# A hybrid convolution and neighbourhood-attention block: another ordering of the same instructions by the framework's scheduler

## The chip, the cores and the metric

The kernel runs on one core of one Trainium2 chip. The metric is the time of one execution on the device in microseconds (us); smaller is better. The engines of the core work in parallel, each through its own list of instructions in order: PE (TensorE: matmuls and transposes), DVE (VectorE: elementwise work), ACT (ScalarE: activations and copies), POOL (GpSimd) and SP (SyncE), the last two here only as issuers of transfers (DMA). An instruction starts when the one ahead of it on its engine is through and the semaphores that it waits for are reached.

## What is computed

One layer over 512 latent tokens of 1024 channels (a grid of 8 rows by 64 columns) with 256 context tokens. Cut to what matters:

```python
h  = _rmsnorm(x, pre_g)   * (1.0 + sc) + sh          # modulation from c
hc = _rmsnorm(ctx, pre_g) * (1.0 + sc_c) + sh_c      # context, modulation from c_ctx
parts = _split_in(h @ w_in)      # 10 parts of 1024: b, c, x_in, z_a, q, k, v, z_b, g_a, g_b
q, k = _apply_rope(_heads(parts[4]), cos, sin), _apply_rope(_heads(parts[5]), cos, sin)
k_c, v_c = split(hc @ w_in[:, K_OFF:V_END])
attn = _neighbourhood_attention(q, k, v, k_c, v_c, rpb)   # window 8 x 16 and all context keys, one softmax
y_a = (silu(z_a) * b * _dwconv3(c * x_in, conv_w, conv_b)) @ w_out_conv
y_b = (silu(z_b) * attn) @ w_out_attn
y   = (sigmoid(g_a) * y_a + sigmoid(g_b) * y_b) @ w_o
return x + gt * _rmsnorm(y, post_g)
```

There are 16 heads of 64 channels; the arithmetic is float32.

## The kernel before

**Precision.** A float32 operand is split in two parts, a high one `H` and a low one `L` (`split`, L64 to L72: ACT casts the high part at L67, or scaled at L70, and DVE takes the difference at L68, or L71). A product is three matmuls: high by high, high by low, low by high. So every weight and every activation costs one pass on ACT and one on DVE ahead of PE.

**Stages.** The prologue (to about 52 us) loads x, computes the modulation from `wmod` (tiles `wm`), transposes the normed x and multiplies the first weight slabs (`fraw`, cast to `fH` and `fL`) as they come: per slab k, ACT makes the modulated `m` (L516), splits it into `h` (L67), and PE multiplies (L422 to L426). For PE, DVE, ACT and SP this part stands inside `manual_schedule`, where the order is that of the code. The load of the rotary tables `cosin` (L554) stands behind that block in the code. Then come four blocks of the convolution branch; then the main part: a loop over 64 blocks (8 head pairs p, two heads h each, four query blocks b), in which each slot issues attention work of pair p and, in between, projection work for later pairs from `plan` (the fillers: `keys_queries`, `values`, `conv_pairs`, `gate2`, `merge_gates`); then the branch projections with the merge (from about 540 us), and the output projection with the closing norm (from about 664 us).

**Attention of one block.** `scores` (L715, or L724 for the fourth block b = 3): PE multiplies queries `qd`, `qe` by keys `ks` into a tile `ps` in one of two banks (`psS`); DVE adds the bias `bt` and takes the row maximum `m` (L731); ACT takes the exponential into `pt` (L738, L742), three buffers in all; after two blocks DVE takes the reciprocal of the sums `z` (L743) and ACT scales both (L745). `turn2` (L752): PE transposes `pt` into two banks (`psT`), and ACT and DVE split the result into `TH` and `TL` (L67, L68). `gather` (L771): twelve matmuls by the values `V` for the whole head; ACT copies (L776), DVE adds into `at` (L777, L778).

**Queries and keys.** `keys_queries` projects q and k for a later pair. For the pairs 3, 4 and 6 (and for some other projections) it goes through `pair` (L293 to L316), which saves multiplications by sums of blocks: products at L287 into three tiles, which ACT copies (L298, L301, L303, L309) and DVE combines (L304, L312, L315) into `tc`. `rope` (L619 to L625) multiplies by the tables on DVE (L621 into `tb`, L622 in place) and adds the swapped half by two accumulating transfers from POOL's queue (L624). After that ACT casts `qd` (L70) and `ks` (L67), and POOL's queue copies halves between tiles (L680, L681, L688 to L690) before the scores of that pair can start. `values` projects v at L175 and L180 (with `summed`, L205 and L206, and the split into `V`); the context's keys are projected at L194 and L199. `block_sums` (L594 to L598) makes the sums `S` of the activations that `pair` multiplies.

**The end.** `tokens` (L1006) multiplies merged activations by blocks of `w_o` for four token tiles t; `squares` (L1027 on ACT, L1028 on DVE) takes the sum of squares and scales; `added` (L1032) adds partial products; `partial` (L1038, L1040) and `close` (L1044 on ACT, L1045 and L1047 on DVE, the output at L1051) finish a tile.

**What sets the order.** Outside `manual_schedule` the code's order is only a proposal. The framework collects the instructions with their dependencies inside `tile.TileContext`, simulates them, and lays down the list of each engine in the order in which its simulation would run them; then it puts in the semaphores. Which simulation it takes is an argument of `TileContext` (L1197).

## Time and profile before

| what | us |
|---|---|
| median of three runs | 709.33 (709.26 to 709.7) |
| the profiled execution | 710.12 |
| its span | 708.3 |
| PE busy | 695.4 |
| DVE busy | 585.2 |
| ACT busy | 437.2 |
| POOL busy | 66.9 |

The profile is of one execution. The span goes from its first to its last instruction; the profiled execution's own time is 1.8 us longer and 0.8 us above the median. The parts that matter are: the busy times; the chain of work that ended last, followed back from the end; the table of what each engine waited for (time in total, times, longest); windows of time with each engine's busy time, PE's granted clock and the share and rate of the DMA engines; and the timeline, whose rows give start, duration, engine, line, operation, output and inputs, a count where equal rows are joined, and in brackets the idle time ahead and who ended it. Matmuls are pipelined, so a row's duration is longer than the distance to the next; prices per matmul are taken from start to start.

### The profile page before, as it was taken

What the parts mean: (1) busy time and instruction counts of PE and PEld (TensorE: products, weight loads), DVE (VectorE), ACT (ScalarE), POOL (GpSimd) and SP (SyncE); (2) the same over time, 40 slices, a digit from 0 to 9 for tenths busy, and PEclk for the clock granted to TensorE, in tenths of its full rate; (3) what the DMA queues carried; (4) which work ended last, traced back from release to release, by engine and by line L of the source; (5) the groups of instructions that cost most, each with busy time, mean ns of one, the idle gap of its engine ahead of it and who ended that gap; (6) DMA issues with size and microseconds to landing.
All of it is one profiled execution on the core that took longest, in us unless ns stands there. A gap on an engine that the chain in (4) does not pass through costs nothing.

```text
span 708.3 us, 11424 instructions
## 1 busy us (share of the span) xinstructions
PE 695.4 (98%) x4196; PEld 618.5 (87%) x4196; DVE 585.2 (83%) x1114; ACT 437.2 (62%) x868; POOL 66.9 (9%) x110
## 2 busy tenths in 40 slices
PE   7999999999999999999999999999999999999996
PEld 4888888888889989898999999999898899988885
DVE  6979997668599989978898797999799675665996
ACT  6566632656577678765886676888694444442563
POOL 0000002240130310401302103000000000000000
PEclk9999999999999999999999999999999999999999
DMA  8996896565341563642636436313733233570013
GB/s 341 407 348 228 281 339 172 134 163 143 100 99 29 137 157 119 151 125 61 168 106 171 94 127 154 104 60 98 250 115 120 88 119 120 186 261 30 31 59 120
DMA packets 37466, 108.27 MB, mean 153 GB/s; under 512 B 5025, under 2 KB 5281, under 8 KB 37410
## 3 DMA queue, kind: packets, MB, share of 16 engines
q1 hardware_dynamic: 28946, 92.20, 38.0%
q0 software_dynamic: 8320, 15.21, 10.7%
q8 instruction: 33, 0.54, 0.3%
q14 instruction: 23, 0.19, 0.1%
q10 hardware_dynamic: 144, 0.13, 0.1%
HBM read 87.07 MB, written 5.24 MB: 130 GB/s over the span
## 4 chain that ended last, share of the span: by engine, by line
PE 88%; DVE 5%; DMA 3%; ACT 2%; issue 1%; SPq 0%; POOL 0%; DVEq 0%; ACTq 0%
PE ps L287 23%; PE ps L162 11%; PE ps L163 11%; PE ps L164 11%; PE ps L175 6%; PE ps L1006 5%; PE ps L771 4%; PE ps L180 3%; PE ps L752 3%; PE ps L715 3%; PE ps L194 2%; PE ps L422 2%; PE ps L426 2%; PE ps L423 2%; DMA fraw<-in_wfirst 1%; DVE w L68 1%
## 5 line engine op out<-in xcount | busy, mean ns | idle before, releaser
L67 ACT CAST w<-raw 128x512 fp32r<-128x512 f32 (+1 forms) x193 | 137.2, 731 | 91.4 <-PE ps L164 30.7
L68 DVE TENSOR_TENSOR w<-raw,w 128x512 fp32r<-128x512 f32 (+1 forms) x193 | 156.3, 824 | 41.8 <-ACT w L67 41.0
L287 PE MATMUL ps<-S,w 128*128 128x256 f32 x960 | 122.0, 283 | 1.2 <-ACT tc L303 1.2
L287 PEld LDWEIGHTS ps<-S,w 128*128 128x128 f32 x960 | 118.1, 192 | 1.5 <-ACT tc L303 1.4
L287 PE MATMUL ps<-h,w 128*128 128x256 f32 x720 | 94.2, 284 | 0.5 <-DVE tc L315 0.4
L287 PEld LDWEIGHTS ps<-h,w 128*128 128x128 f32 x720 | 89.9, 191 | 2.5 <-DVE tc L315 0.9
L162 PE MATMUL ps<-h,w 128*128 128x512 f32 x208 | 81.5, 392 | 0.0
L164 PE MATMUL ps<-h,w 128*128 128x512 f32 x208 | 81.2, 390 | 0.0
L163 PE MATMUL ps<-h,w 128*128 128x512 f32 x208 | 81.0, 390 | 0.0
L624 POOL DMA_DIRECT2D tc<-tb x32 | 28.8, 1175 | 301.9 <-DVE tc L622 182.6
L164 PEld LDWEIGHTS ps<-h,w 128*128 128x128 f32 x208 | 39.0, 188 | 8.2
L67 ACT CAST TH<-ps 128x512 fp32r<-128x512 f32 x64 | 36.0, 588 | 16.5 <-PE ps L752 16.4
L162 PEld LDWEIGHTS ps<-h,w 128*128 128x128 f32 x208 | 39.1, 188 | 8.0
L163 PEld LDWEIGHTS ps<-h,w 128*128 128x128 f32 x208 | 39.1, 188 | 7.9
L731 DVE CUSTOM_DVE_ANT_1 ps<-ps,bt 128x512 f32<-128x512 f32 x56 | 38.8, 694 | 8.4 <-PE ps L715 8.2
L745 ACT ACTIVATE pt<-pt,z 128x512 f32<-128x512 f32 x64 | 42.9, 721 | 4.6 <-DVE z L743 4.3
L68 DVE TENSOR_TENSOR TL<-ps,TH 128x512 fp32r<-128x512 f32 x64 | 42.4, 681 | 0.8 <-ACT TH L67 0.7
L752 PE MATMUL ps<-ident,pt 128*128 128x128 f32 x256 | 33.2, 273 | 0.0
L175 PE MATMUL ps<-w,h 128*128 128x512 f32 x128 | 32.3, 394 | 0.0
L752 PEld LDWEIGHTS ps<-ident,pt 128*128 128x128 f32 x256 | 29.3, 140 | 2.1
L738 ACT ACTIVATE pt<-ps,m 128x512 f32<-128x512 f32 x32 | 22.0, 689 | 10.8 <-DVE m L731 10.0
L771 PE MATMUL ps<-TH,V 128*128 128x256 f32 (+1 forms) x96 | 28.4, 318 | 0.0
(249 smaller groups left out, 1387.6 us busy)
## 6 DMA issues: line engine op xcount, KB each, us to landing
raw<-in_win SPq DMA_DIRECT2D x74, 512.0 KB, 4.5
wm<-in_wmod SPq DMA_DIRECT2D x34, 512.0 KB, 6.4
raw<-in_wout SPq DMA_DIRECT2D x16, 512.0 KB, 3.8
bt<-in_rel SPq DMA_DIRECT2D x16, 256.0 KB, 3.0
tc<-tb POOLq DMA_DIRECT2D x32, 128.0 KB, 3.8
B<-in_wo SPq DMA_DIRECT2D x8, 512.0 KB, 7.4
fraw<-in_wfirst SPq DMA_DIRECT2D x8, 384.0 KB, 8.7
qd<-qd POOLq DMA_DIRECT2D x24, 128.0 KB, 2.4
```

The lines of the kernel that those rows point to most:

```text
L67: nc.scalar.copy(H, src)
L68: nc.vector.tensor_sub(L, src, H.bitcast(F32))
L162: nc.tensor.matmul(ps, lhsT=H[k][:, cs], rhs=mH[k], start=k == 0, stop=False)
L163: nc.tensor.matmul(ps, lhsT=H[k][:, cs], rhs=mL[k], start=False, stop=False)
L164: nc.tensor.matmul(ps, lhsT=L[k][:, cs], rhs=mH[k], start=False, stop=k == KT - 1)
L175: nc.tensor.matmul(ps, lhsT=mH[k][:, ts], rhs=both[k].rearrange("p a c -> p (a c)"), start=k == 0, stop=False, skip_group_check=True,)
L287: nc.tensor.matmul(ps, lhsT=w[:, x, k], rhs=act[y][k], start=start and k + o == 0, stop=k == 3 and o == 2, skip_group_check=True,)
L731: nc.vector.tensor_tensor_reduce(out=s3, in0=s3, in1=bt[:, e::4 - e][:, 0:2], scale=-1.0, scalar=3.0e38, op0=ALU.add, op1=ALU.min, accum_o ...
L745: nc.scalar.mul(x, x, z[:, i:i + 1])
L752: nc.tensor.transpose(tp[:, c], pt[:, c * P:(c + 1) * P], ident)
L771: nc.tensor.matmul(o3[:, dst], lhsT=V[p][:, kt, h], rhs=src(t), start=n == 0 and t is TH, stop=n == len(work) - 1 and t is TL,)
L1006: nc.tensor.matmul(out, lhsT=a(x, k, ts), rhs=w[y][k // 2][:, k % 2, cols], start=start and k + o == 0, stop=k == 3 and o == 2, skip_group ...
```

## The change

```diff
@@ -1194,7 +1194,7 @@
-    with tile.TileContext(nc) as tc:
+    with tile.TileContext(nc, schedule_with_timeline_sim=True) as tc:
         layer(tc, **args)
```

The scheduler takes its timeline simulation in place of its default one to order the instructions of every engine. The instructions themselves are the same, as are the tiles, buffers and banks; the semaphore waits follow the order. What is inside `manual_schedule` keeps its order on PE, DVE and ACT; on SP the load of `cosin` moves into it. Elsewhere nearly every stretch of each list is arranged anew. Three places are shown.

PE, around the second head of pair 1 and the first head of pair 2 (numbers in the names tell tiles apart: `ps_2207`, `ps_2221` and `ps_2334` are three scores tiles in a row, `ps_2231` and `ps_2232` transposes, `ps_2182` a tile of the values projection). Before:

```order
L180 MATMUL ps_2182<-w_1830,hc2_92 128x256 x2
L180 MATMUL ps_2182<-w_1830,hc3_93 128x256 x2
L715 MATMUL ps_2207<-ks_1895,qd_1891 128x512
L715 MATMUL ps_2207<-ks_1895,qe_1893 128x512
L715 MATMUL ps_2221<-ks_1895,qd_1891 128x512
L715 MATMUL ps_2221<-ks_1895,qe_1893 128x512
L752 MATMUL ps_2231<-ident_73,pt_2052 128x128 x4
L752 MATMUL ps_2232<-ident_73,pt_2131 128x128 x4
L287 MATMUL ps_2258<-h0_82,w_2057 128x256 x3
```

Of the change (`ps_2030` is the gather of the head before; the transposes `ps_2136` of `pt_1936` stand twelve rows ahead of `ps_2137`):

```order
L771 MATMUL ps_2030<-TL_1828,V_1163 128x256
L752 MATMUL ps_2137<-ident_73,pt_1944 128x128 x4
L180 MATMUL ps_2158<-w_1830,hc3_93 128x256 x2
L715 MATMUL ps_2221<-ks_1895,qd_1891 128x512
L715 MATMUL ps_2221<-ks_1895,qe_1893 128x512
L752 MATMUL ps_2231<-ident_73,pt_2052 128x128 x4
L715 MATMUL ps_2334<-ks_1895,qd_1891 128x512
L715 MATMUL ps_2334<-ks_1895,qe_1893 128x512
L175 MATMUL ps_2182<-w_1829,hc0_90 128x512 x2
```

The third scores tile `ps_2334` now stands ahead of the projection `ps_2182`, where before it stood thirty-five rows behind it; the first, `ps_2207`, stands ahead of `ps_2158`. On ACT, what stands between the exponential into the buffer that `pt_1936` leaves (`pt_2131`) and the one that frees the bank for `ps_2334` (`pt_2212`) is, of the change:

```order
L742 ACTIVATE pt_2131,z_2053<-ps_2124,m_2129 128x512
L67 CAST S23_2215<-tc_2150 128x512
L745 ACTIVATE pt_2052<-pt_2052,z_2053 128x512
L745 ACTIVATE pt_2131<-pt_2131,z_2053 128x512
L67 CAST S43_2218<-tc_2151 128x512
L67 CAST TH_2055<-ps_2136 128x512
L776 COPY ta_2043<-ps_2030 64x512
L205 COPY ta_2093<-ps_2076 128x256
L67 CAST TH_2055<-ps_2137 128x512
L738 ACTIVATE pt_2212,z_2213<-ps_2207,m_2210 128x512
```

Before, both TH casts stood ahead of the first of these exponentials, and casts of values and weights stood in their place between the two.

DVE, the rotary of pair 3 (`tc_2256` is its q, `tc_2257` its k; `w_` are weight splits, `ps_2408`, `ps_2464` and `ps_2551` scores of pair 2, `TL_2343` the low part of transposed probabilities). Before:

```order
L312 SCALAR_TENSOR_TENSOR tc_2257<-tc_2257,ps_2260 128x256
L315 TENSOR_TENSOR tc_2256<-tc_2256,ps_2259 128x256
L731 ISA ps_2408,m_2413<-ps_2408,bt_1039 128x512
L731 ISA m_2413 128x1
L621 TENSOR_TENSOR tb_2398<-tc_2256,cosin_80 128x512
L621 TENSOR_TENSOR tb_2403<-tc_2257,cosin_80 128x512
L622 TENSOR_TENSOR tc_2256<-tc_2256,cosin_80 128x512
L622 TENSOR_TENSOR tc_2257<-tc_2257,cosin_80 128x512
```

Of the change, from the second of the two score rows that stand there now (ahead of it stand L312, a weight split, L315, the scores `ps_2464` and another weight split):

```order
L731 ISA ps_2551,m_2554<-ps_2551,bt_1039 128x512
L731 ISA m_2554 128x1
L68 TENSOR_TENSOR TL_2343<-ps_2421,TH_2342 128x512
L621 TENSOR_TENSOR tb_2398<-tc_2256,cosin_80 128x512
L621 TENSOR_TENSOR tb_2403<-tc_2257,cosin_80 128x512
L68 TENSOR_TENSOR TL_2343<-ps_2561,TH_2342 128x512
L743 RECIPROCAL z_2470<-z_2470 128x2
L206 TENSOR_TENSOR ta_2458<-ta_2458,ps_2441 128x256
L622 TENSOR_TENSOR tc_2256<-tc_2256,cosin_80 128x512
L68 TENSOR_TENSOR w_2485<-raw_2314,w_2485 128x512
L622 TENSOR_TENSOR tc_2257<-tc_2257,cosin_80 128x512
```

The four rotary passes were adjacent; now attention and weight work of other tiles stands between them and ahead of them.

PE, the last matmuls of the kernel (`ps_7248` is token tile 2, `ps_7535` the first and `ps_7249` the second half of the last columns of tile 3). Before:

```order
L1006 MATMUL ps_7248<-w_7461,A22_7202 128x512 x3
L1006 MATMUL ps_7248<-w_7461,A23_7203 128x512 x3
L1006 MATMUL ps_7535<-w_7460,A20_7200 128x256 x3
L1006 MATMUL ps_7535<-w_7460,A21_7201 128x256 x3
L1006 MATMUL ps_7535<-w_7461,A22_7202 128x256 x3
L1006 MATMUL ps_7535<-w_7461,A23_7203 128x256 x3
L1006 MATMUL ps_7249<-w_7460,A20_7200 128x256 x3
```

Of the change:

```order
L1006 MATMUL ps_7535<-w_7461,A22_7202 128x256 x3
L1006 MATMUL ps_7535<-w_7461,A23_7203 128x256
L1006 MATMUL ps_7248<-w_7460,A20_7200 128x512 x3
L1006 MATMUL ps_7248<-w_7460,A21_7201 128x512 x3
L1006 MATMUL ps_7248<-w_7461,A22_7202 128x512 x3
L1006 MATMUL ps_7248<-w_7461,A23_7203 128x512 x3
L1006 MATMUL ps_7535<-w_7461,A23_7203 128x256 x2
L1006 MATMUL ps_7249<-w_7460,A20_7200 128x256 x3
```

Ten of the twelve matmuls of `ps_7535` moved ahead of the last twelve of `ps_7248`; the last two and all of `ps_7249` stay at the end. On DVE both L1047 of tile 2 moved behind L1040 of tile 3, and the last L1028 and L1045 stand behind these.

## The prediction

> **What bounds the kernel now.** I read the page first, then the waits of TensorE, the windows of 20 us, and the timelines of the places where PE waits or where the order changes most.
>
> ```profile
> span 708.3 us, 11424 instructions
> PE 695.4 (98%) x4196; PEld 618.5 (87%) x4196; DVE 585.2 (83%) x1114; ACT 437.2 (62%) x868; POOL 66.9 (9%) x110
> PE 88%; DVE 5%; DMA 3%; ACT 2%; issue 1%; SPq 0%; POOL 0%; DVEq 0%; ACTq 0%
> ```
>
> PE is busy 98% of the span and is 88% of the chain that ended last. The other engines matter where they make PE wait. The waits of PE, with us in total, times and longest:
>
> ```profile
> PE ps L470 <- ACT crow L442: 3.4, 1, 3.4
> PE ps L422 <- ACT h L67: 1.2, 1, 1.2
> PE ps L287 <- ACT tc L303: 1.2, 1, 1.2
> PE ps L287 <- DVE tc L315: 0.4, 1, 0.4
> ```
>
> The first two lie in the prologue, whose order on PE, DVE and ACT is written out by hand and stays. The last two, 1.2 + 0.4 = **1.6 us**, are all that a better order inside the kernel could take from these rows. Where they are is seen in the windows (PE busy is the first number behind the length, the clock stands ahead of the DMA share):
>
> ```profile
> 20.00:40.00 20.00, 20.00 (x99) 16.38 (x98) 20.00 (x36) 10.63 (x15) 0.00 (x0) 1.00 1.03 406
> 220.00:240.00 20.00, 20.00 (x148) 18.90 (x147) 18.88 (x43) 16.29 (x38) 0.00 (x0) 1.00 0.20 56
> 240.00:260.00 20.00, 18.36 (x142) 17.31 (x141) 16.81 (x36) 14.13 (x31) 8.22 (x13) 1.00 0.69 159
> 260.00:280.00 20.00, 19.91 (x158) 19.11 (x157) 19.07 (x40) 15.73 (x35) 0.00 (x0) 1.00 0.32 116
> 480.00:500.00 20.00, 19.93 (x158) 19.10 (x158) 17.18 (x35) 15.37 (x32) 0.00 (x0) 1.00 0.46 143
> 700.00:709.00 9.00, 2.06 (x18) 1.86 (x16) 4.85 (x12) 1.58 (x6) 0.00 (x0) 0.90 0.32 117
> ```
>
> From 240 to 260 PE lacks 1.64 us, and it ends at 702.06. Everywhere else between 20 and 700 us it lacks under 0.1 in 20. An order that is only different therefore has little to win and much to lose: DVE is busy 18.88 of 20 us from 220 to 240, so a step that is asked for early there finds no free time. The cause of the 1.2 us, from the timeline and, in the second fence, the chain in order of time:
>
> ```profile
> 239.87 1.29 DVE L622 TENSOR_TENSOR tc<-tc,cosin 128x512 f32<-128x512 f32 x2
> ...
> 249.75 0.62 ACT L67 CAST ks<-tc 128x512 fp32r<-128x512 f32 x1 [3.87 <-DMA tc<-tb]
> ...
> 250.97 3.13 PE L287 MATMUL ps<-S,w 128*128 128x256 f32 x24 [1.21 <-ACT tc L303]
> ```
>
> ```profile
> 242.80 6.88 DMA tc<-tb
> ```
>
> The rotary of pair 3 ends on DVE at 239.87 + 1.29 = 241.16; its last transfer is issued at 242.80 and lands at 249.7. ACT stands at the key cast for 3.87 us, in order, with the PSUM copies of L301 and L303 behind it, and PE waits for these.
>
> **The change, part by part.** The instructions are the same; only their order and waits differ. So nothing is paid for instructions, and the sum has only waits.
>
> *More changes of group on PE.* The new order cuts accumulations up: the runs of matmuls into one output tile and line go from 575 to 681 by the two orders. What a change costs:
>
> ```profile
> 236.48 0.40 PE L724 MATMUL ps<-ks,qd 128*128 128x256 f32 x2
> ...
> 236.96 1.03 PE L752 MATMUL ps<-ident,pt 128*128 128x128 f32 x8
> ...
> 237.75 2.08 PE L194 MATMUL ps<-hc,w 128*128 128x512 f32 x8
> ...
> 239.68 1.12 PE L199 MATMUL ps<-hc,w 128*128 128x256 f32 x8
> ...
> 240.63 0.40 PE L715 MATMUL ps<-ks,qd 128*128 128x512 f32 x1
> ```
>
> From start to start, four matmuls of 256 columns take 0.48 us (0.12 each), eight transposes 0.79 (0.10), eight of 512 columns 1.93 (0.24), eight of 256 columns 0.95 (0.12), across a change each time. A change costs nothing beyond 0.00 to 0.01 us; 106 more cost 0 to 1 us, and I take **0**. The granted clock was 1.00 in all these windows. [...]
>
> *Attention ahead of its filler, near 220 us.* The new order puts the scores of three blocks (L715), the transposes (L752) and the rest of a gather (L771) close together, and pulls products of the values projection between and behind them. Three buffers `pt` serve the softmax. The exponential of the fourth block can't start before the transposes of the first have left PE, and on ACT there now stand behind those transposes: an exponential with its sum, two S casts, two scalings, two TH casts, the L776 copy, an L205 copy and the next exponential; only then is the bank of the third scores tile free. ACT's prices at this place (timeline):
>
> ```profile
> 217.84 0.70 ACT L742 ACTIVATE pt<-ps,m 128x512 f32<-128x512 f32 x1
> 218.42 0.21 ACT L742 ACTIVATION_READ_ACCUMULATOR pt<-ps,m 128x1 f32 x1
> 219.09 1.34 ACT L745 ACTIVATE pt<-pt,z 128x512 f32<-128x512 f32 x2 [0.47 <-DVE z L743]
> 220.34 0.35 ACT L205 COPY ta<-ps 128x256 f32<-128x256 f32 x1
> 220.59 1.14 ACT L67 CAST S<-tc 128x512 fp32r<-128x512 f32 x2
> 223.86 0.69 ACT L738 ACTIVATE pt<-ps,m 128x512 f32<-128x512 f32 x1
> 225.60 1.06 ACT L67 CAST TH<-ps 128x512 fp32r<-128x512 f32 x2
> 231.92 0.58 ACT L776 COPY ta<-ps 64x512 f32<-64x512 f32 x1 [0.30 <-PE ps L771]
> ```
>
> The exponential with its sum is 218.63 - 217.84 = 0.79, and the whole 0.79 + 1.14 + 1.34 + 1.06 + 0.58 + 0.35 + 0.69 = 5.95 us. Neighbours overlap by about 0.1 (219.09 to 220.34 holds 1.34 in 1.25), five times over: 5.4. PE has in the same stretch three wide and eight narrow matmuls of L771, eight transposes, two narrow of L180 and two wide of L715: 5 x 0.24 + 10 x 0.12 + 8 x 0.10 = 3.2. PE waits 5.4 - 3.2 = **2.2 us**; at most 2.8 without overlap, at least 0, where ACT comes there with other work done earlier. In the order before, two whole groups of the values projection stood in this stretch and covered ACT.
>
> *The rotary of pair 3, 236 to 252 us.* Between the last L312 and the last L622 the new DVE order has three weight passes, a second score row in place of one, two TL passes more, a reciprocal and an L206: six passes of 128x512 net and two short ones. The page gives a pass of that size:
>
> ```profile
> L731 DVE CUSTOM_DVE_ANT_1 ps<-ps,bt 128x512 f32<-128x512 f32 x56 | 38.8, 694 | 8.4 <-PE ps L715 8.2
> tc<-tb POOLq DMA_DIRECT2D x32, 128.0 KB, 3.8
> ```
>
> 6 x 0.69 + 0.5 = 4.6, less overlap 4.3 us. Count from the last product that L312 needs (236.48 before): the rotary ended 4.7 behind it and would end 9.0 behind it. The last transfer was issued 1.6 after that end; by the median of 3.8 us it lands at 9.0 + 1.6 + 3.8 = 14.4, by the 6.88 of the chain at 17.5. ACT then has the key cast, a weight cast, an exponential and L301, 0.62 + 0.6 + 0.9 + 0.36 = 2.5 us. PE has before its first need of L301 eighteen wide, eighty narrow and twenty transposes, 18 x 0.24 + 80 x 0.12 + 20 x 0.10 = 15.9. The wait is 14.4 + 2.5 - 15.9 = 1.0, or 4.1 by the long transfer. I take **2.0**, nearer the median since the 6.88 is the longest of 32. It takes the place of the 1.6 us of before, which I count as **-1.6**.
>
> *The other pairs (280 to 530 us).* Scores move ahead by some us in pairs 4 to 7 too, with PE's 20.00 or 19.93 of 20 now. I bound it by 0 and two more waits of the kind above, 4.4, and take **1.0**, under half of one.
>
> *The prologue's queue.* SP now issues the `cosin` load (512 KB) ahead of the later slabs: 512 KB at the window's 406 GB/s are 1.3 us on each later one. What covers it:
>
> ```profile
> 27.11 0.62 ACT L67 CAST h<-m 128x512 fp32r<-128x512 f32 x1
> ...
> 29.50 0.47 PE L422 MATMUL ps<-h,fH 128*128 128x512 f32 x1
> ```
>
> ACT has the fourth slab's cast at 27.73, PE asks for it at 29.50: 1.8 us. So **0**, at most 1.3 if that cover were used up.
>
> *The end.* Ten narrow matmuls of token tile 3's first half now stand ahead of the last twelve of tile 2, so tile 2 is complete 10 x 0.12 = 1.2 us later, while PE ends at the same time.
>
> ```profile
> 699.29 0.60 ACT L1027 ACTIVATE cs<-ps 128x512 f32<-128x512 f32 x1 [0.71 <-PE ps L1006]
> ...
> 700.01 0.69 DVE L1028 TENSOR_TENSOR ys<-ps,gpost 128x512 f32<-128x512 f32 x1 [1.24 <-ACT cs L1027]
> ...
> 701.01 1.41 DVE L1047 SCALAR_TENSOR_TENSOR ys<-ys,sums,xr 128x512 f32<-128x512 f32 x2
> ...
> 703.44 1.54 DVE L1047 SCALAR_TENSOR_TENSOR ys<-ys,sums,xr 128x512 f32<-128x512 f32 x3
> ```
>
> L1028 of tile 2 starts at 701.2; behind it on DVE stand L1028 of tile 3, two tiny steps, the two L1047 of tile 2, and only then the last L1028. 701.2 + 0.6 + 0.35 + 0.15 + 1.3 + 0.35 + 0.15 = 704.1 against 703.44: **+0.6**, between 0 and 1.2.
>
> The sum on the profiled execution of 710.12 us (span 708.3 and 1.8 around it): 710.12 - 1.6 + 2.2 + 2.0 + 1.0 + 0 + 0 + 0.6 = 714.3. That execution is 0.8 above the median of 709.33, so I predict **713.5 us**, 4.2 over the runs shown.
>
> **The rivals.** *The new order covers its waits (faster).* At the rotary of pair 3 PE has 15.9 us of work ahead of its need, where before it had 250.97 - 1.21 - 236.48 = 13.3. With the landing of before, 13.3 behind the same point, ACT is through at 15.8 and the wait is gone. That decides if the rotary ends no later than before, or under 3 us later with a median landing, and if ACT arrives at 220 with 2 us in hand. Then 709.33 - 1.6 = 707.7. Against it speak nine more rows on a DVE that is nearly full.
>
> *One of the two waits is covered.* The rest (1 to 2 us, less 1.6, with the end's 0.6) cancels: 708.5 to 710.7.
>
> *The waits repeat in each paired stage* (pairs 4 and 6 have the same rotary): two more of 2.2 and one of the long kind, 713.5 - 1.0 + 2 x 2.2 + 4.1 = 721. For it speaks that DVE and ACT have the same work there; against it that PE showed no wait at all in these windows before.
>
> *The order changes nothing* (a row apart here and there): 709.3. The two orders differ in nearly all of PE's rows, so this is unlikely.
>
> *The clock falls.* PE could run slower behind a wait. In the trace 1.64 us of idle left the clock at 1.00; a longer wait inside the kernel isn't shown. Were PE at half speed behind each new wait for as long as the wait itself, that would add (2.2 + 2.0 + 1.0) / 2 = 2.6: 716.1. [...]
>
> **How the numbers follow.** Forecast (711 to 718): 0.55. Covered: 0.12. One covered: 0.13. Repeated: 0.14. No change: 0.03. Clock: 0.03. The range starts at 708.0, inside the covered case, and ends at 721.0, at the repeated case, which leaves about 2 in 10 out. A measurement of this kernel tells 0.2%, 1.4 us, from no change. Below 707.9 lies nearly all of the covered case: 0.11. Within 1.4 us lie one covered, no change and the rest: 0.17. Above: 0.72.
>
> **What would show it.** In the profile of the changed kernel the waits of PE should have a row of L715 or L752 on ACT or DVE of about 2 us near 220, and one of L287 on ACT L301 or L303 of 1 to 4 us near 255; the window from 220 to 240 should show PE below 20.00. The prologue's first two waits should stay. The last L1047 should start some 2 us behind PE's end, where it was 703.44 - 702.06 = 1.4. If PE shows 20.00 in all windows from 200 to 280, the argument on ACT and DVE is wrong; if the loss lies in stages beyond 280, my allowance of 1.0 was.

## The result, and the profile after

| | before | after |
|---|---|---|
| median | 709.52 us (4 runs, 709.26 to 710.0) | 718.03 us (4 runs, 717.7 to 719.26) |
| profiled execution | 710.12 | 717.92 |
| its span | 708.3 | 716.1 |

The ratio is 1.0122, with a 95% interval of 1.011 to 1.0135: the changed order is 8.5 us slower, where 4.2 were forecast. The direction and the kind of loss (new waits of PE) were right, and the time lies inside the range; the size was half of what was measured.

The head of the page of after, and the chain that ended last by engine:

```profile
span 716.1 us, 11502 instructions
PE 698.9 (98%) x4196; PEld 620.2 (87%) x4196; DVE 583.8 (82%) x1114; ACT 435.6 (61%) x868; POOL 66.8 (9%) x110
PE 90%; DVE 4%; DMA 3%; ACT 2%; issue 1%; DVEq 0%; SPq 0%; ACTq 0%
```

The work is the same: as many busy instructions on each engine (the 78 more in the head only handle semaphores), DVE and ACT a little less busy than before. PE is *more* busy by 3.5 us with the same 4196 matmuls; a slower clock, shown below, makes 1.5 of it, and the rest was not traced. The waits of PE in after (us in total, times, longest):

```profile
PE ps L470 <- ACT crow L442: 3.4, 1, 3.4
PE ps L287 <- ACT tc L301: 2.6, 2, 1.6
PE ps L752 <- DVE TL L68: 2.1, 1, 2.1
PE ps L287 <- ACT g L301: 0.8, 2, 0.6
PE ps L422 <- ACT h L67: 0.4, 1, 0.4
PE ps L162 <- ACT g L309: 0.4, 1, 0.4
PE ps L715 <- ACT pt L738: 0.3, 1, 0.3
```

The prologue's rows are still there. The rows of L303 and L315 are gone, and five new ones stand in their place, 6.2 us in all against 1.6. Where they lie, by windows (length, busy PE, PEld, DVE, ACT, POOL with counts, then PE's granted clock, DMA share, GB/s):

```profile
220.00:240.00 20.00, 17.60 (x119) 16.02 (x118) 16.58 (x40) 17.12 (x43) 0.00 (x0) 0.91 0.21 67
240.00:260.00 20.00, 18.39 (x138) 17.29 (x138) 18.28 (x40) 13.16 (x30) 6.46 (x10) 1.00 0.46 115
340.00:360.00 20.00, 19.04 (x144) 17.92 (x143) 16.12 (x33) 12.94 (x29) 6.43 (x11) 1.00 0.62 141
480.00:500.00 20.00, 19.35 (x158) 18.83 (x157) 20.00 (x41) 15.62 (x33) 0.00 (x0) 1.00 0.21 67
500.00:520.00 20.00, 19.60 (x132) 17.98 (x131) 16.82 (x29) 15.74 (x28) 0.00 (x0) 1.00 0.69 238
520.00:540.00 20.00, 19.68 (x137) 17.96 (x136) 19.13 (x41) 12.25 (x23) 0.00 (x0) 1.00 0.26 85
```

From 220 to 240 PE starts 119 matmuls where it started 148, and the clock is 0.91. In shorter windows of 3.41 us, the length of the stretch at half clock:

```profile
220.69:224.10 3.41, 1.35 (x7) 1.06 (x8) 3.26 (x9) 3.36 (x9) 0.00 (x0) 1.00 0.00 0
224.10:227.51 3.41, 3.41 (x11) 2.64 (x10) 2.97 (x10) 2.92 (x9) 0.00 (x0) 0.50 0.00 0
227.51:230.92 3.41, 3.41 (x31) 3.41 (x31) 2.73 (x7) 3.40 (x9) 0.00 (x0) 1.00 0.01 2
```

In the first PE is busy for 1.35 us only, and all through the second its clock is 0.50.

The timeline there shows the wait and the half clock behind it:

```profile
217.64 0.69 ACT L742 ACTIVATE pt<-ps,m 128x512 f32<-128x512 f32 x1 [4.53 <-PE ps L752]
...
222.44 0.63 PE L752 MATMUL ps<-ident,pt 128*128 128x128 f32 x4 [2.09 <-DVE TL L68]
...
223.38 0.50 PE L715 MATMUL ps<-ks,qd 128*128 128x512 f32 x1 [0.31 <-ACT pt L738]
...
223.94 3.47 PE L175 MATMUL ps<-w,hc 128*128 128x512 f32 x8
```

ACT first stands idle for 4.53 us until PE's transposes are through; then everything that stands behind on ACT and DVE is late, and PE waits 2.09 + 0.31 = 2.4 us for it. Then eight wide matmuls take 3.27 us from start to start (223.94 to 227.21), where the price before was 1.93. The second place, near 257:

```profile
250.01 0.68 DVE L622 TENSOR_TENSOR tc<-tc,cosin 128x512 f32<-128x512 f32 x1
250.03 3.56 POOL L624 DMA_DIRECT2D tc<-tb  x4 [40.59 <-ACT pt L745]
...
257.19 0.62 ACT L67 CAST ks<-tc 128x512 fp32r<-128x512 f32 x1 [1.08 <-DMA tc<-tb]
...
258.91 0.36 ACT L301 COPY tc<-ps 128x256 f32<-128x256 f32 x1
...
259.32 2.41 PE L287 MATMUL ps<-S,w 128*128 128x256 f32 x18 [1.61 <-ACT tc L301]
```

The rotary ends at 250.69, the key cast gets its transfer at 257.19, and the L301 copy stands behind it. The third, near 350:

```profile
343.32 2.48 SPq L87 DMA_DIRECT2D raw<-in_win  x2
...
350.07 0.62 ACT L67 CAST w<-raw 128x512 fp32r<-128x512 f32 x1 [3.70 <-DMA raw<-in_win]
...
353.18 3.01 PE L287 MATMUL ps<-S,w 128*128 128x256 f32 x23 [0.96 <-ACT tc L301]
```

Here ACT, in order, stands 3.70 us at a *weight* cast whose transfer was issued 6.7 us earlier, with attention's casts and the L301 copy behind it. Of all profiles only this one shows this third loss (see mend_350).

**Where the 7.8 us of span came from.** For each profile I took the moment at which PE had done the same amount of matmul work (each matmul at its usual distance to the next: 0.23, 0.12 and 0.10 us for 512, 256 and 128 columns), and the lag behind before at that moment. Prices 2% apart move the values by at most 0.1 us. The columns are moments of before (the rows below after are experiments, told further on). What stands at 213 comes from the prologue, whose length differs a little between executions:

| lag, us | 213 | 225 | 256 | 300 | 340 | 356 | 478 | 545 | 701 |
|---|---|---|---|---|---|---|---|---|---|
| after | -0.3 | 4.2 | 4.6 | 3.4 | 3.4 | 4.8 | 4.8 | 7.0 | 7.1 |
| raw_first | -0.3 | 2.5 | 5.0 | 4.3 | 4.3 | 4.3 | 4.3 | 9.8 | 9.8 |
| keep_busy_220 | -0.4 | 2.5 | 4.5 | 4.3 | 4.3 | 4.3 | 4.3 | 6.0 | 6.0 |
| rope_early | -0.1 | 4.0 | 3.1 | 1.9 | 1.9 | 1.9 | 1.9 | 3.8 | 3.8 |
| loop_open | -0.1 | 1.0 | 4.6 | 4.1 | 4.1 | 4.2 | 4.2 | 6.4 | 6.4 |
| mend_all | -0.3 | 0.9 | 2.5 | 1.3 | 1.3 | 1.3 | 1.4 | 6.7 | 6.7 |
| mend_four | -0.4 | 0.7 | 1.6 | 0.4 | 0.4 | 0.5 | 0.5 | 2.6 | 2.6 |
| mend_to_470 | -0.7 | 0.5 | 1.6 | 0.4 | 0.4 | 0.4 | 0.7 | 0.6 | 0.6 |

After loses 4.4 near 220, gets 0.8 back by 300, loses 1.4 at 350 and 2.3 from 478 to 545. raw_first has the order of after up to about 500 us, so its row is a second execution of that order: it loses less near 220 and more near 257, and nothing at 350. Behind PE's end stand 716.1 - 709.12 = 7.0 us instead of 708.3 - 702.06 = 6.2: another 0.7.

### The profile page after: what moved, and what is told of

It reads as the page before. It is cut to its first block, busy times and chain, and to the rows that moved or that the text cites. A ratio compares the mean times of both kernels' runs of the same rounds, so it can differ in the third digit from the quotient of the medians.

```text
span 716.1 us, 11502 instructions
## 1 busy us (share of the span) xinstructions
PE 698.9 (98%) x4196; PEld 620.2 (87%) x4196; DVE 583.8 (82%) x1114; ACT 435.6 (61%) x868; POOL 66.8 (9%) x110
## 4 chain that ended last, share of the span: by engine, by line
PE 90%; DVE 4%; DMA 3%; ACT 2%; issue 1%; DVEq 0%; SPq 0%; ACTq 0%
PE ps L287 25%; PE ps L164 10%; PE ps L162 10%; PE ps L163 10%; PE ps L175 6%; PE ps L1006 5%; PE ps L771 4%; PE ps L752 4%; PE ps L180 3%; PE ps L715 3%; PE ps L194 2%; PE ps L422 2%; DMA raw<-in_win 2%; PE ps L426 2%; PE ps L423 2%; PE ps L724 1%
## 5 line engine op out<-in xcount | busy, mean ns | idle before, releaser
L287 PE MATMUL ps<-S,w 128*128 128x256 f32 x960 | 126.9, 284 | 3.5 <-ACT tc L301 2.6
L287 PEld LDWEIGHTS ps<-S,w 128*128 128x128 f32 x960 | 120.6, 191 | 6.7 <-ACT tc L301 3.1
L287 PE MATMUL ps<-h,w 128*128 128x256 f32 x720 | 95.1, 284 | 0.0
L287 PEld LDWEIGHTS ps<-h,w 128*128 128x128 f32 x720 | 90.5, 191 | 1.0
L162 PE MATMUL ps<-h,w 128*128 128x512 f32 x208 | 81.6, 393 | 0.4 <-ACT g L309 0.4
L162 PEld LDWEIGHTS ps<-h,w 128*128 128x128 f32 x208 | 39.1, 188 | 8.5 <-ACT g L309 0.6
L752 PE MATMUL ps<-ident,pt 128*128 128x128 f32 x256 | 36.6, 272 | 2.1 <-DVE TL L68 2.1
L752 PEld LDWEIGHTS ps<-ident,pt 128*128 128x128 f32 x256 | 29.7, 140 | 4.0 <-issue 2.5
L175 PE MATMUL ps<-w,h 128*128 128x512 f32 x128 | 32.8, 393 | 0.0
L771 PE MATMUL ps<-TH,V 128*128 128x256 f32 (+1 forms) x96 | 28.9, 322 | 0.0
```

The lines of the kernel that those rows point to most:

```text
L162: nc.tensor.matmul(ps, lhsT=H[k][:, cs], rhs=mH[k], start=k == 0, stop=False)
L175: nc.tensor.matmul(ps, lhsT=mH[k][:, ts], rhs=both[k].rearrange("p a c -> p (a c)"), start=k == 0, stop=False, skip_group_check=True,)
L287: nc.tensor.matmul(ps, lhsT=w[:, x, k], rhs=act[y][k], start=start and k + o == 0, stop=k == 3 and o == 2, skip_group_check=True,)
L752: nc.tensor.transpose(tp[:, c], pt[:, c * P:(c + 1) * P], ident)
L771: nc.tensor.matmul(o3[:, dst], lhsT=V[p][:, kt, h], rhs=src(t), start=n == 0 and t is TH, stop=n == len(work) - 1 and t is TL,)
```

## The experiments

All have the same instructions (keep_busy_220 has 16 more). An order is imposed by edges between neighbours on an engine that only order. "Stretch" kernels take a piece of every engine's list from one order and the rest from the other; moments are those of the order that a piece is from. The runs of before beside them had medians of 709.28 to 709.87.

**Is it the stretch near 220?**

```diff
 every engine: order of before
-205 to 236: before
+205 to 236: after
```

> The order of before with only the stretch from 205 to 236 us in the changed order. Theory (the loss at 220 is made by this stretch's order alone, whatever comes ahead or behind): the wait of 2.1 + 0.3 us and the half clock come back, and the time is 709.5 + 4.4 = 713.9, less up to 1 us if the later waits of before at 250 and 258 us get shorter because their transfers were asked for earlier against PE. Rival (the wait comes from work that arrives late from ahead of the stretch): a wait under 1 us, 709.5 to 711.

Measured: 713.75 us (712.86 to 715.52), ratio 1.0064 [1.0047, 1.0081], the number that was expected, by a path that was not. The same waits come back (2.09 + 0.33), this time with the eight L175 in 2.01 us and a clock of 1.00 from 220 to 240; the half clock comes later, behind a wait of 2.65 at L303 (0.91 in the window from 240 to 260). So this stretch alone makes half of the loss, partly by what it makes late behind it. The reverse:

```diff
 every engine: order of after
-205 to 236: after
+205 to 236: before
```

> The changed order, but the stretch from 205 to 236 us in the order of before. Theory (the loss there is this stretch's order on PE, ACT and DVE together: scores and transposes ahead of the values projection, so that one buffer or bank after the other isn't free): no wait and clock 1.00 there, 718.0 - 4.4 = 713.6; the wait at 257 us on L301 may grow by up to 1 us since PE gets there earlier against the rotary's transfers, and may then bring its own half clock of 1.7: up to 716.3. Rival (the wait only moves to the next scarce buffer, as in the run with the TH cast moved): over 717.

Measured: 719.34 us (718.21 to 720.37), 1.0145 [1.0129, 1.016]: no gain, the rival's number. The waits moved to the seams (1.87 at 209, 2.03 at 243) and to 260 (2.44). As I read it, a stretch in another order leaves other rows unfinished at its ends, so that this run says little on the stretch itself.

**Two cuts, at 300.** After up to 300 and then before, and the reverse:

```diff
 every engine
-after
+after to 303, then before
```

> The changed order up to 303 us of its own profile, from there the order of before. The two profiles at equal work of PE differ by 3.3 us at this point and by 7.0 at PE's end, with 0.7 more behind it. Theory (the losses are local waits that add up): 709.5 + 3.3 = 712.8. Rival (losses at the start give slack to what follows, or the early losses are absorbed): under 711.5; rival (the waits behind 303 us come from what was done earlier, so they stay): over 715.

Measured: 714.0 us (712.49 to 714.81), 1.0062 [1.0047, 1.0077]: 1.2 above what was expected; 3.2 of lag stands at 340 and 3.7 at the end.

```diff
 every engine
-after
+before to 300, then after
```

> The order of before up to 300 us, the changed order from there. By the two profiles at equal work of PE the changed order loses 3.9 us from 300 us to PE's end (1.4 near 350, 0.6 near 487, 1.9 from 500 to 540) and 0.7 behind it. Theory (these losses are made by the order of the later stages alone): 709.4 + 4.6 = 714.0. Rival (they are aftereffects of the late arrival from the stages ahead): under 711.5.

Measured: 712.9 us (712.22 to 713.38), 1.0049 [1.0036, 1.0062], 1.1 below what was expected. The lag grows from 0.2 at 300 to 2.1 at the end, nearly all from 478 to 545, and 0.7 lie behind PE's end. The step at 350 is *not* there, though the cast stands where it does in after.

**The end alone.**

```diff
 every engine
-before
+before to 664, then after
```

> The order of before up to 664 us, the output projection and the end in the changed order. Theory (the end costs the 0.7 us by which the stretch from PE's end to the last transfer differs between the two profiles, because tile 2 is complete 1.2 us later): PE ends as before, 702.1 us, and the time is 709.4 + 0.7 = 710.1. Rival (the longer end came only from the later arrival of earlier work): 709.4.

Measured: 710.35 us (709.53 to 711.2, 10 runs), 1.0012 [1.0003, 1.0021]: +0.9, of which the trace shows 0.7 behind PE's end.

**What the wait near 220 hangs on.** Three attempts on one or two engines. First, ACT and DVE do the TH and TL of the first transposes ahead of the sums' casts:

```diff
 ACT
 L742 pt_2131<-ps_2124
+L67 TH_2055<-ps_2136
-L67 S23_2215
 L745 pt_2052
 L745 pt_2131
-L67 S43_2218
-L67 TH_2055<-ps_2136
 ...
 L742 pt_2226<-ps_2221
+L67 S23_2215
+L67 S43_2218
 DVE: L68 TL_2056<-ps_2136 ahead of L731 ps_2221, the passes of S behind the second L68 TL_2056
```

> The changed order with one place rearranged: on ScalarE the TH cast of the transposes ps_2136 right behind the exponential into pt_2131 and the two S casts behind the exponential into pt_2226, on VectorE the TL pass of ps_2136 ahead of the scores ps_2221 and the two S passes behind the second TL pass. Theory (the 220-us loss of 4.4 us is a wait of 2.4 us that this queueing makes, and 2.0 us of half clock that the wait brings on): the waits of L752 and L715 there fall under 0.5 us, the clock stays at 1.00 from 224 to 228, and the time falls from 718.0 by 4.0 to 4.4, to 713.6 to 714.0. Rival (the slow clock from 224 to 228 has another cause, such as the kind of work there): the wait goes, the clock still falls, and the time is 715.6 to 716.0.

Measured: 719.45 us (717.73 to 720.12), 1.0137 [1.0122, 1.0153]. Neither theory had that time. The wait didn't go but moved by two rows: 0.23 at L752, then 1.96 at L715, for the bank that ACT's exponential frees. The weaker form:

```diff
 ACT
-L67 S23_2215
-L67 S43_2218
 L742 pt_2226<-ps_2221
+L67 S23_2215
+L67 S43_2218
 DVE: the passes of S behind the second L68 TL_2056
```

> The changed order with only the two S casts and the two S passes moved back at 220 us, TH and TL staying behind the scalings. The wait of L752 should fall from 2.1 us by the two casts, 1.1 us, to about 1.0. Theory (the clock falls only after a long wait; 1.6 us at 257 us left it at 1.00): clock 1.00 from 224 to 228 and a time of 718.0 - 1.1 - 2.0 = 714.9. Rival (the slow clock lasts in proportion to the wait): half of it stays, 718.0 - 1.1 - 1.0 = 715.9. Rival (the slow clock has another cause): 716.9.

Measured: 717.24 us (715.63 to 719.06), 1.0109 [1.0086, 1.0132]. That is above all three expected times. The wait is 1.49 + 0.22, where 1.0 was expected, and the clock is again 0.91 from 220 to 240. Third, on PE alone:

```diff
 PE
+L752 ps_2136 x4
+L771 ps_2030 (rest of the gather)
 L180 ps_2158
 ...
-L752 ps_2136 x4
-L771 ps_2030
```

> The changed order with one move on PE: the transposes ps_2136 and the rest of the gather ps_2030 ahead of the values projection ps_2158. In the changed kernel ACT stands idle for 4.5 us (213.1 to 217.6) at the exponential whose buffer those transposes free, and then PE waits 2.4 us for what is queued behind it on ACT and DVE. Theory (the pair of waits is one loop through the three pt buffers, the one TH tile and the banks, opened by PE's order): ACT's idle time falls under 1.5 us, PE's wait at 220 under 0.6 us, clock 1.00; 718.0 - 2.5 to 4.1 = 713.9 to 715.5, the lesser gain if PE waits longer at 257 us. Rival (the stretch from 200 to 260 us is bound by what ACT and DVE have to do there, so that PE only waits later): 717 or more.

Measured: 716.64 us (716.25 to 718.22), 1.0108 [1.0092, 1.0123], between theory and rival. ACT's idle time shrank from 4.53 to 2.79 and 0.53, yet PE waits as long as in after. DVE shows why:

```profile
220.30 0.70 DVE L731 CUSTOM_DVE_ANT_1 ps<-ps,bt 128x512 f32<-128x512 f32 x1 [1.85 <-PE ps L715]
...
220.91 0.69 DVE L68 TENSOR_TENSOR S<-tc,S 128x512 fp32r<-128x512 f32 x1
221.52 0.68 DVE L68 TENSOR_TENSOR TL<-ps,TH 128x512 fp32r<-128x512 f32 x1
```

DVE stands 1.85 us at scores that PE has not made yet, with the TL pass that PE will wait for behind them. So the three engines wait for one another in a ring, and opening one link leaves the next. With all moved together:

```diff
+PE: as in ahead_220
+ACT, DVE: as in no_wait_220
```

> The changed order with both rearrangements near 220 together: on PE the transposes ps_2136 and the rest of the gather ps_2030 ahead of the projection ps_2158, on ACT the TH cast of ps_2136 ahead of the S casts and scalings, on DVE the TL pass of ps_2136 ahead of the scores ps_2221 and the S passes behind the second TL. Theory: each rearrangement alone left PE waiting 2 us because the next scarce buffer's release still stood late on another engine; with the three engines moved together the wait near 220 is under 0.5 us, the clock stays at 1.00 there, and the time is 718.0 - 4.4, plus up to 2 us given back by a longer wait and a fall of the clock near 257: 713.6 to 715.6 us. Rival: ACT and DVE lack the time for the work that is asked of them there whatever its order, PE waits 1.5 to 2.5 us at another tile, and the time is 716.5 to 719.5.

Measured: 717.23 us (715.51 to 718.1), 1.0105 [1.0091, 1.0119], the rival's number. From the timeline of loop_open:

```profile
221.16 0.50 PE L715 MATMUL ps<-ks,qd 128*128 128x512 f32 x1 [0.22 <-ACT pt L738]
...
222.28 2.11 PE L175 MATMUL ps<-w,hc 128*128 128x512 f32 x8 [0.39 <-DVE ta L206]
...
258.58 4.63 PE L287 MATMUL ps<-S,w 128*128 128x256 f32 x24 [2.63 <-ACT tc L301]
```

The 2.4 us of waiting are 0.6 now, so near 220 the order made most of the wait, rather than a lack of time on ACT or DVE. The lag at 225 falls by 3.2 (4.2 to 1.0), but 0.8 of it is lost again by 235, and 1.5 is the half clock, which raw_first escapes there with the whole wait. The next wait, near 257, is 2.63 in place of 1.61, and now the clock falls behind *it* (0.97 from 240 to 260 and 0.94 from 260 to 280; 24 narrow matmuls take 4.63 us, 3.13 in before): PE comes there 1.8 us earlier than in after, and the key cast, which stands ahead of the L301 copy and waits for the rotary's transfer, only 0.7 (256.45 and 257.19). So PE is no earlier at 300 than in after (lag 4.1 and 3.4), and of the repair 0.8 us of time are left (718.03 - 717.23, with overlapping intervals).

**Is the half clock PE's own idleness?** The order of after, with 16 transposes added that compute the four blocks of `ps_2137` four times more, in the wait near 220:

```diff
 PE
 L715 ps_2221<-ks_1895,qe_1893
+L752 ps_2137<-ident_73,pt_1944 128x128 x16
 L752 ps_2231<-ident_73,pt_2052
```

> The changed order with sixteen more transposes on PE, which write the same values into ps_2137 once more (their line is L758, lines behind L752 are 2 to 6 higher) and stand where PE waits 2.1 us at 220 us; they take 1.6 us of that wait and end ahead of the ACT cast that reads ps_2137. Theory (the half clock from 224 to 227.5 comes from PE's idleness, and costs 2.0 us of the 4.4): clock 1.00 there, the same wait in all, and a time of 718.0 - 2.0 = 716.0, or down to 717 where PE meets the later wait at 257 us earlier. Rival (the slow clock comes from something else at this place): 718.0, with the windows from 224 to 228 as slow as they were.

Measured: 716.61 us (716.08 to 717.68), 1.0105 [1.009, 1.0119], as expected. The added work is L758 in its timeline, and lines behind it are shifted (L754 is L752):

```profile
220.09 1.91 PE L758 MATMUL ps<-ident,pt 128*128 128x128 f32 x16
222.34 0.63 PE L754 MATMUL ps<-ident,pt 128*128 128x128 f32 x4 [0.34 <-DVE TL L68]
223.35 0.50 PE L715 MATMUL ps<-ks,qd 128*128 128x512 f32 x1 [0.39 <-ACT pt L738]
...
223.92 1.98 PE L175 MATMUL ps<-w,hc 128*128 128x512 f32 x8
```

The next rows start as late as in after (223.92, 223.94), but the eight wide ones take 1.98 instead of 3.47, at a clock of 1.00 (220 to 240). That is not yet the work of the added transposes: raw_first (below) has the same order here, nothing added, and the whole wait, and keeps the clock as well:

```profile
222.36 0.63 PE L752 MATMUL ps<-ident,pt 128*128 128x128 f32 x4 [2.09 <-DVE TL L68]
...
223.86 2.01 PE L175 MATMUL ps<-w,hc 128*128 128x512 f32 x8
...
258.78 4.55 PE L287 MATMUL ps<-S,w 128*128 128x256 f32 x24 [2.65 <-ACT tc L301]
```

So the same rows behind the same wait ran once at half clock (after) and once at full clock (raw_first): the kind of work there is not the reason, and the half clock near 220 cost 1.5 us when it came. Where it didn't come, PE met the wait near 257 earlier, waited longer there (2.65 here, 2.62 in keep_busy_220) and the clock fell then (0.95 from 260 to 280 here, 0.93 in keep_busy_220). The four profiles with the unmended order up to 300 us (after, after_then_before, mend_350, raw_first) have one such fall each before 300, three near 220 and one near 257. The time of keep_busy_220 came out as expected for another reason than the one given, which is luck: at 300 us PE is later than in after (4.3 and 3.4), and the gain of 1.4 (the two intervals overlap a little) comes from the step at 350, which is missing, and from 478 to 545.

**A wait planted into before,** by two casts ahead of the L301 and L303 copies of pair 3:

```diff
 ACT
+L67 CAST w (the next one)
+L67 CAST TH (the next one)
 L301 COPY tc
 L303 COPY tc
```

> The order of before with one edit: on ScalarE the copies L301 and L303 of pair 3 stand behind one weight cast and one TH cast more, which lengthens PE's wait at 250 us from 1.2 by 1.1 to about 2.3 us and changes nothing else. Theory (a wait of about 2 us lowers PE's clock to half for some 3.4 us, in most executions, which costs 1.7 us more): 709.4 + 1.1 + 1.7 = 712.2, single times spread over 1.7 us, granted clock near 0.5 in a window behind 252 us. Rival (a wait costs its length): 710.5, with times as close together as those of before.

Measured: 710.32 us (708.84 to 711.17, 11 runs), 1.0012 [1.0003, 1.0021]: the rival's number. The mechanism is the theory's, though: the wait is 2.35, and the clock, which stays at 1.00 there in before, falls behind it (0.91 from 240 to 260; 23 narrow matmuls take 4.37 us, where 24 took 3.13). So a wait put in by hand brought the fall. But the lag, 2.0 at 256, is 0.9 at 300 and 0.4 at the end: the order of before has slack behind it.

**Before without its two waits:**

```diff
 ACT: L67 ks behind L301 and L303
 DVE: L315 right behind the first L312
```

> The order of before with its two waits taken out by order alone: on ScalarE the cast of ks, which waits 3.9 us for the rotary's transfer, stands behind the copies L301 and L303, on VectorE L315 stands right behind the first L312. Theory (both waits are work queued behind something that waits): the waits of 1.2 and 0.4 us go, with the latencies around them 1.4 + 0.6, and the time is 709.4 - 1.9 = 707.5. Rival (the keys then come too late for their scores, or another wait takes their place): 709 to 710.

Measured: 709.98 us (708.94 to 711.42, 11 runs), 1.0009 [1.0, 1.0018], the rival's number. The rows of 1.2 and 0.4 are gone, and L771 on TH (1.2), L287 on L298 (0.7) and L771 on TL (0.4) stand in their place.

**The rotary of pair 3 alone:**

```diff
 DVE
 L315 tc_2256<-tc_2256,ps_2259
+L621 tb_2398
+L621 tb_2403
+L622 tc_2256
+L622 tc_2257
 ...
-L621 tb_2398
-L621 tb_2403
-L622 tc_2256
-L622 tc_2257
```

> The changed order, but on DVE the four rotary passes of pair 3 (two L621, two L622) stand adjacent, right behind its L315, as they did before. If the wait of 1.6 us on the L301 copy near 257 comes from the late end of the rotary on DVE (its last transfer then lands behind the key cast's turn on ACT), the rotary ends some 4 us earlier, the wait goes, and the time is 718.0 - 1.6 = 716.4 us; with executions in which the clock also falls behind that wait, down to 715. Rival: the passes that are now behind the rotary (scores and TL) hold PE up instead, and the time stays within 0.7 us of 718.0 or rises.

Measured: 714.39 us (712.97 to 716.93), 1.0071 [1.0054, 1.0087]: 3.6 faster than after, where 1.6 were expected. From its timeline:

```profile
245.60 1.29 DVE L622 TENSOR_TENSOR tc<-tc,cosin 128x512 f32<-128x512 f32 x2
246.83 3.56 POOL L624 DMA_DIRECT2D tc<-tb  x4 [37.21 <-DVE tc L622]
...
249.46 0.63 PE L752 MATMUL ps<-ident,pt 128*128 128x128 f32 x4 [0.35 <-DVE TL L68]
...
256.98 0.36 ACT L301 COPY tc<-ps 128x256 f32<-128x256 f32 x1
```

PE has no wait at L287 any more, though the wait of 2.09 at 220 is still there, with a clock of 0.91. By the lag at 300 this gives 1.5 (3.4 to 1.9), about what was expected. The step at 350 is missing too (lag 1.9 and 1.9): the weight transfer that ACT waited 3.70 us for is there after 0.62, with the same orders at that place. That is 1.4 more, which is not the rotary's.

**The cast at 350 alone:**

```diff
 ACT
-L67 CAST w<-raw (the one that waits for its transfer)
 L67 CAST TH x2
 L67 CAST ks
 L742
 L301 COPY tc
+L67 CAST w<-raw
 DVE: its L68 pass behind the second L68 TL
```

> The changed order with one cast moved at 350 us: ACT's weight cast w<-raw that stands 3.7 us idle for its transfer goes behind the two TH casts, the ks cast, an exponential and L301, and its DVE pass behind the second TL. Theory (PE's loss of 1.4 us from 351 to 353 is head-of-line waiting of ACT at a transfer): the L771 and L301 delays there go, 718.0 - 1.4 = 716.6. Rival (it moves to the next use): 717.5 to 718.

Measured: 715.53 us (715.05 to 717.32), 1.0093 [1.0077, 1.011]. The step is missing (lag 3.0 at 340, 3.0 at 356), but this run doesn't show that the move took it away. Its weight load landed 3.7 us after its issue, against 6.7 in after. And in nine other profiles with the cast in its old place (no_wait_220, half_wait, ahead_220, undo_220, loop_open, keep_busy_220, raw_first, rope_early, before_then_after) the cast waited only 0.6 to 2.4 us, and the lag grew by 0.1 or less. So the order puts ACT's other work behind that transfer, but the 1.4 us were lost only in the one execution in which it came late. Whether the three other runs of after lost them is not known, nor what makes this run 2.5 us faster than after, where 1.4 were expected.

**One load on SP:**

```diff
 SP
+L87 raw_5938<-in_win
 L887 ur0_5850<-usc0_94
 ... (seven more L887, two L889)
-L87 raw_5938<-in_win
```

> The changed order, but on SP the weight load raw_5938 ahead of the eight ur loads, as it stood before. If ACT's waits for raw tiles of 1.8 to 2.1 us near 505 to 510 are what costs PE its 1.5 us between 505 and 545, the lag of PE there goes down by 0.4 (its wait on the g copy at 511.67) to 1.5 us: 716.5 to 717.6. Rival: other rows of that stage make PE late (its own order, the as cast behind the tb transfer), and the time stays within 0.5 us of 718.0.

Measured: 720.86 us (719.39 to 721.96), 1.0158 [1.0144, 1.0171]: 2.8 *slower*, which neither theory had. From its timeline:

```profile
512.59 0.62 ACT L67 CAST us<-ur 128x512 fp32r<-128x512 f32 x1 [3.81 <-DMA ur<-usc]
513.11 0.36 ACT L309 COPY g<-ps 128x256 f32<-128x256 f32 x1
...
513.53 0.50 PE L162 MATMUL ps<-h,w 128*128 128x512 f32 x1 [2.80 <-ACT g L309]
```

In ACT's list of after, the first cast of `us` stands ahead of the L309 copy. With the weight load ahead, the `ur` transfers start later, ACT stands at that cast, and PE waits behind the copy, with a clock of 0.91 from 500 to 520. By this reading the load would have to be moved together with ACT's rows; that was not run.

**All together:**

```diff
+edits of loop_open, rope_early, mend_350 and raw_first
-every engine from 664: after
+every engine from 664: before
```

> The changed order with all mends together: near 220 (as loop_open), the rotary of pair 3 early (as rope_early), the weight cast at 350 later (as mend_350), the load raw_5938 ahead of the eight ur loads on SP, and everything from 664 on in the order before. If the loss is the sum of separate places, the time is 718.0 - 4.4 - 0 to 1.6 - 1.4 - 0.5 to 1.5 - 0.7 = 709 to 711 us. Rival: a PE that is made to wait less at one place arrives earlier at the next one and waits there; then 713 us or more.

Measured: 717.08 us (716.77 to 717.88), 1.0108 [1.0094, 1.0121]: the rival's side, and the lag tells where: 1.7 at 505, and 6.3 at 520, again the `us` cast (PE waits 2.7 at L162, and the clock falls behind it, 0.91 from 500 to 520). So the next run is the same without the edit on SP (its expectation reckons with 0.9 and 5.4 in place of 1.7 and 4.6):

```diff
 mend_all
-edit of raw_first
```

> As mend_all, but SP keeps the changed order (raw_5938 behind the ur loads). If the 5.4 us that PE lost in mend_all between 505 and 520 (ACT standing at the us cast for the ur transfer, with the g copy behind it) came from that load's place alone, PE is 0.9 us behind the order before at 505, loses the 1.2 to 2.4 us that the changed order lost there in the other runs, and the time is 709.9 + 2.1 to 3.3 = 712.0 to 713.2 us. Rival: PE arrives earlier at that stage whatever SP does, and waits there; then 715 or more.

Measured: 712.68 us (711.96 to 714.06), 1.0053 [1.004, 1.0065], as expected. And with the order of before from 470 on:

```diff
 mend_four
-every engine from 470 to 664: after
+every engine from 470 to 664: before
```

> As mend_four up to 470, and the order before from there on. If the loss between 480 and 545 is made by the changed order of that stretch, it goes: PE is 0.4 to 1.2 us behind the order before at 470 and stays there, 710.3 to 711.1 us. Rival: a seam or the earlier or later arrival of the transfers costs the same 1.2 to 2.4 us, and the time is that of mend_four, 712 or more.

Measured: 711.17 us (710.58 to 711.95), 1.003 [1.0019, 1.0041], just above what was expected. mend_four and mend_to_470 differ from 470 to 664 alone: that stretch costs 1.5 us. No version beat before. What mend_to_470 still waits for inside the kernel:

```profile
PE ps L752 <- DVE TL L68: 1.6, 1, 1.6
PE ps L422 <- ACT h L67: 1.2, 1, 1.2
PE ps L175 <- DVE ta L206: 0.4, 1, 0.4
```

The first is the transposes at 248, with TL passes of DVE late; as I read it, the rotary passes that now stand ahead of them are the reason, and this is the price of rope_early.

## Where the prediction failed and where it held

Two steps failed. The term for the other pairs was taken as 1.0 us and came to 3.7, and the fall of the clock behind the new waits, put at nothing in the sum, came to 1.5. Against its own profiled execution the forecast was 714.3; after's is 717.92, 3.6 more. By its terms:

- **More changes of group: 0.** Right as far as the runs tell: from 60 to 200 us, where the groups are cut up too, after's lag stays between -0.28 and -0.25.
- **Near 220: +2.2.** The wait was 2.09 + 0.31 = 2.4, at L752 and L715 as said. The counting of ACT's rows gave the right number, with one thing not seen: ACT comes there after 4.53 us of idle time, and DVE has its own part in the ring (ahead_220). loop_open shows that the order made most of the wait.
- **The clock: not in the sum.** This step failed. "In the trace 1.64 us of idle left the clock at 1.00" was carried over to waits of 2 us and more; the case got a chance of 0.03. In after the fall cost 3.27 - 1.93 = 1.34 us on L175 and 0.14 on the eight L180 behind it. plant_wait shows the fall behind a wait of 2.35 put in by hand, and raw_first that it can come at the next wait instead. The rival's half speed for as long as the wait was the author's assumption; in after the clock was 0.50 for 3.41 us behind a wait of 2.4.
- **The rotary of pair 3: +2.0 in place of 1.6.** The mechanism is as said, and nearly every number: the rotary ends 9.1 us behind its last product (9.0 forecast), the transfer lands 6.5 us behind that end (5.4 taken), ACT needs 2.1 for the key cast to L301 (2.5), PE has 16.1 of work until its need (15.9), and waits 1.61 at L301. rope_early shows the cause. The net from 225 to 300 is -0.8 instead of +0.4: from start to start, three pauses cost before 1.37 + 0.59 + 0.25 = 2.2 us there, of which the prediction counted 1.6, and one costs after 1.8; the other 0.4 are spread over spacings under 0.1 us and were not settled. With a full clock at 220 the same order waits 2.65 (raw_first).
- **The other pairs: +1.0.** The step that was most mis-sized: 7.1 - 3.4 = 3.7 us from 300 to the end of PE, 1.4 at 350 and 2.3 from 478 to 545. The bound of 4.4 held, the value "under half of one" wait did not. The kind was wrong too: what was looked for was scores drawn ahead, and what came was ACT, in order, at a cast that waits for a weight's transfer (350), and waits for g copies on ACT (480 to 545). The first is in one profile alone, so its size is that of one late transfer. The second is made by the order of that stretch: before_then_after has it, and mend_to_470 against mend_four is worth 1.5 us. Which of its rows make it is open; the one row that was moved by itself, in raw_first, was not it.
- **SP's cosin: 0.** Right: the lag at 213 is -0.3, so PE leaves the prologue no later.
- **The end: +0.6.** 0.7, and the last L1047 starts 711.26 - 709.12 = 2.1 us behind PE's end, as said.

The sum of the differences: clock 1.5, near 220 0.2 and some 0.5 of small gaps there, pair 3 -1.2, other pairs 2.7, end 0.1, prologue -0.3: 3.5 of the 3.6.

Of the rivals, "the waits repeat" had the right place for the rest (later stages) but the wrong kind, and "the clock falls" the right kind at too low a chance. The covered case is refuted by the rows of L752 and L301.

## What to carry to other kernels

Where PE is busy 98% of the span, as here, another order of the same instructions has little to win, and it lost where an in-order engine stood at an instruction whose input was late (a transfer, or PE itself) with a pass behind it that PE needed: look in the new lists for casts of loaded data ahead of PSUM copies, and not only where PE's own rows moved. Read the granted clock behind a wait of PE: here it fell behind ten of eleven waits of 2.35 to 2.80 us, and a fall cost 1.5 us. And count such places together: a repair that put PE 3 us ahead at 225 left nothing of it at 300, since PE then came earlier to the next late input, while a planted loss of 2.3 us cost 0.9. Read a second execution, too, before a single wait is put down to the order: the 1.4 us at 350 stood in one profile of ten.

## What the hardware showed that was not expected

**The clock fell to 0.50 behind some waits of PE and not behind others.** In after the granted clock is 0.50 from 224.10 to 227.51 and 1.00 on both sides. A stretch of 3.41 us at 0.50 stands also in half_wait (from 222.87 and from 260.42), in rope_early (from 222.83) and in raw_first (from 514.62). In the 3.41 us ahead of these five, PE was busy for 1.35 us in after, 1.70 and 1.00 in half_wait, 1.32 in rope_early and 1.09 in raw_first. Behind windows of the same length with 1.72 and 2.68 in only_220, 1.81 and 2.61 in raw_first and 2.33 in after (from 258.24) it stayed at 1.00; these are laid in steps of 3.41 us from a fall of the same execution. The two nearest to each other, first half_wait:

```profile
219.46:222.87 3.41, 1.70 (x11) 1.05 (x10) 2.46 (x7) 3.36 (x8) 0.00 (x0) 1.00 0.00 0
222.87:226.28 3.41, 3.41 (x9) 2.64 (x10) 2.81 (x8) 3.41 (x10) 0.00 (x0) 0.50 0.00 0
```

And only_220:

```profile
218.55:221.96 3.41, 1.72 (x13) 1.28 (x12) 2.67 (x7) 3.36 (x7) 0.00 (x0) 1.00 0.00 0
221.96:225.37 3.41, 2.68 (x13) 2.13 (x14) 3.24 (x10) 3.41 (x11) 0.00 (x0) 1.00 0.00 0
```

In after most of the wait of 2.09 + 0.31 lies in a window with 1.35; in raw_first it is spread over two, and the clock stayed at 1.00:

```profile
217.66:221.07 3.41, 2.61 (x19) 2.09 (x17) 1.94 (x6) 3.41 (x7) 0.00 (x0) 1.00 0.03 12
221.07:224.48 3.41, 1.81 (x9) 1.43 (x10) 3.26 (x8) 3.36 (x10) 0.00 (x0) 1.00 0.00 0
```

Single times of a kernel with such waits lie up to 4 us apart (712.97 to 716.93 in rope_early), but those of before lie up to 2.3 apart too, so the times by themselves don't show it. Counted from 200 us on: behind the wait of 2.09 at L752 near 220 the clock fell in four profiles (after, after_then_before, mend_350 and rope_early, 0.91 each from 220 to 240) and stayed at 1.00 in three (raw_first, only_220 and ahead_220). Ten of eleven waits of 2.35 to 2.80 were followed by a fall, in nine profiles; the 2.44 of undo_220 was not. Among the shorter ones the 1.49 + 0.22 of half_wait was, but not the 1.61 of after, the 1.5 to 1.6 of mend_all, mend_four and mend_to_470, the 1.96 of no_wait_220 or the 1.87 and 2.03 of undo_220. So the length of a wait alone doesn't tell; what else the clock goes by was not tested by kernels made for it. A fall cost 1.5 us (1.34 + 0.14 in after, 4.63 - 3.13 in loop_open). For the forecast wait of 2.2 the four of seven give, as an estimate, 4/7 x 1.5 = 0.9 us on the mean. keep_busy_220 tests nothing here, since raw_first kept the clock without the added work too.

**The same load took 3.7 to 6.7 us:** the weight load near 343 landed 6.7 us behind its issue in after, and 3.7 to 5.4 us behind it in the 13 other profiles that have the changed order there. An accumulating transfer of the rotary was started 1.3 us ahead of it in after, but that alone is not the reason: in ahead_220, keep_busy_220, raw_first and mend_350 it was started 0.8 to 1.0 us ahead, and the load landed in 3.7 to 4.0. The reason stays open.
